# First 128 prompt tokens as a first group, with their expert rows gathered beside the recurrence

## The chip, the cores and the metric

The kernel runs on one core of a Trainium2 chip. The metric is device time in microseconds (us) of one execution, as the median of several runs. TensorE (PE in the profile) multiplies matrices, VectorE (DVE), ScalarE (ACT) and GpSimd (POOL) work on elements, SyncE (SP) issues most transfers; GpSimd issues the indirect ones. Each engine works through its own list of instructions in order; semaphores tie the lists together.

## The reference

One layer of a hybrid decoder is computed for 1024 prompt tokens and 32 sample tokens, 1024 features wide, in 32-bit floats:

```python
n1 = rmsnorm(x, norm_mix_g);  z = n1 @ w_in
y_r, shift_new, wkv_new = rwkv7_mix(z[..., :D_SHIFT], ...)   # 8 heads of 64; a scan over the tokens
y_p, pool_new = pool_mix(z[..., D_SHIFT:], ...)              # windows of 2, 4, 8, 16 tokens
h = x + concat([y_r, y_p]) @ w_out
h = h + peer_ffn(rmsnorm(h, norm_ffn_g), wq, keys, u_tab, v_tab)
gate = sigmoid(rmsnorm(h, norm_ple_g) @ ple_gate_w)
h = h + (p @ ple_w) * gate
y = rmsnorm(h, final_norm_g)

def peer_ffn(x):            # per token: 8 heads, 16 of 16384 experts each
    s1, s2 = q[:, :, 0] @ keys[0].T, q[:, :, 1] @ keys[1].T   # q = x @ wq
    v1, i1 = top_k(s1, 16);  v2, i2 = top_k(s2, 16)
    sc, ci = top_k(v1[..., :, None] + v2[..., None, :], 16)
    gate = softmax(sc)
    act = gelu(u_tab[expert] . x) * gate
    return sum(act * v_tab[expert])
```

The outputs are y for both kinds of tokens and the new shift, recurrence and pooling states.

## The kernel before

The 1056 tokens stand in one order of positions, the 32 samples first. Matrix products that need full precision split both operands into a high and a low part (`whi`, `wlo`, `yhi`, `ylo`) and do three passes.

Phase A projects all tokens through `w_in`, prepares the recurrence's inputs in `fd`, and makes the pooled features `yp_d`. Beside it, `wsplit` loads, splits and stores `wq` and the first half of `w_out`, in 40 half blocks, each through one buffer `sraw`. The recurrence (`bchunk`) takes the prompt in 16 chunks of 64 tokens, each handing a state `S` to the next (L613), with two chunks interleaved (`b_stream`); a chunk's masked factors are made on POOL (`ltm`, `X`), and its output goes to `y_d`. The samples have a chunk of their own.

After chunk 1, with the next chunks and the sample chunk merged in, `ple` (the embedding projection to `pl_d`) and `wpool` (the pooled half of `w_out` plus `x`, to `hx_d`) run for all tokens. Then the four token groups of `GROUPS` follow, 288, 256, 256 and 256 positions. `phase_c(gi)` does a group's output projection (TensorE passes at L661 to L663, then L704), norm (L718), `wq` (16 blocks) and key scores, which go to memory. `top` reads them back and finds the top 16 of each half, and `select` (inside `top`) the experts and gates.

The expert layer is done in two ways. Positions 0 to 671 (`GA` to `GB`) are dense: every expert row of `uT` and `vP` is applied to them in 128 blocks of 128 experts (L1075 through `ublock` and `vblock`, weights split at L1061 and L1063), each token's gates standing in a dense tile. `select` builds that tile in 168 steps of four tokens: two comparisons and products on VectorE (L875, L877, some on L878 or POOL), eight TensorE passes (L881), an eviction (L882); 32 tokens at a time go from `gst` to `g_d`. The other 384 positions (`GT`) are gathered in three tiles of 128 tokens: for each of 8 heads and 16 experts an indirect DMA (L1179) fetches one row of `u` per token, VectorE takes its product with the token (L1187), and after gelu and gate another fetches a row of `v`, which VectorE adds to `po` (L1196). Four `row` buffers take turns.

```python
for gi ... streams = [phase_c(step - 1), t_stream(step - 2), b_stream(...)]; merge(streams)
for col in range(0, GT, 128):       # top of the gather tiles, then the dense blocks,
    idx, gl = tinfo[GB + col]       # and each gather tile in turn
```

`merge` interleaves streams by their shares of steps done, `BC` says which chunks go with which group. What order each engine really gets is decided by a scheduler that works on its own estimate of the time; the tile pools with their buffer counts (`bufs`) set the waits. `gates` (in `Tail`) does the embedding gate at the end, for the dense part and then for the gathered one (`GH`), and `finish` writes `yT`.

Of the kernel before, what the change touches and what calls it, by code (L numbers as in the profile page):

```python
# [40 lines left out]
GROUPS = ((0, 288), (288, 544), (544, 800), (800, 1056))  # L41
# [20 lines left out]
def body(ctx, tc, io):  # L62
# [12 lines left out]
    hx_d = dram.tile([128, KB, T], F32, name="hx_d")  # L75
# [30 lines left out]
    keep = ctx.enter_context(tc.tile_pool(name="keep", bufs=1))  # L106
# [4 lines left out]
    pconst = phases.enter_context(tc.tile_pool(name="pconst", bufs=1))  # L111
# [8 lines left out]
    pbx = ExitStack()  # L120
# [44 lines left out]
    keys = pconst.tile([128, 2, 128], F32)  # L165
# [288 lines left out]

    maxn = max(b - a for a, b in GROUPS)
    def bchunk(c, sp=None):
# [7 lines left out]
        pos = 0 if smpl else NSMP + 64 * c  # L464
# [83 lines left out]
        def sample_s(k, o, last):  # L548
            for p in range(4):
                apb = sp[0][0].tile([128, NB, m], F32, name="apb", bufs=2)  # L550
# [42 lines left out]
        if smpl:  # L593
            po = out()
            for p in range(4):
                ps = PS(pst)
                for i, (k, s_) in enumerate(((1, vt), (0, u))):
                    uvb = sp_.tile([m, NB, 64], F32, name="uvb", bufs=2)
# [42 lines left out]
    def wblock(gi, b):  # L641
# [4 lines left out]
        for i in range(1 if b < KB else 2):  # L646
# [25 lines left out]
    def segs(gi):  # L672
        c0, c1 = GROUPS[gi]
        if c0 == 0:
            return ((0, NP, NSMP), (NSMP, 0, c1 - NSMP))
        return ((0, c0 - NSMP, c1 - c0),)
# [5 lines left out]
    def phase_c(gi):  # L682
# [7 lines left out]
        y = work.tile([128, 4, maxn], F32, name="y", tag="yp")  # L690
        nc.sync.dma_start(y[:, :, :n], y_d[:, :, c0:c1])
# [80 lines left out]
    def select(tk, col, m, V12, I12):  # L772
# [133 lines left out]

    def t_stream(gi):
        for t0, m in tiles_of(gi):
            if GA <= GROUPS[gi][0] + t0 < GB:
                yield from top(tk, GROUPS[gi][0] + t0, m)  # L910

    def t_len(gi):
        n = 0
        for t0, m in tiles_of(gi):
            if GA <= GROUPS[gi][0] + t0 < GB:
                n += 24 + m // 4
        return n
# [11 lines left out]
    BC = (0, 2, 4, 8, 12, 16)  # L929
# [23 lines left out]
    with tc.tile_pool(name="smp", bufs=1) as sp_, tc.tile_pool(name="hx", bufs=1) as hx:  # L953
# [17 lines left out]
        pT = sp_.tile([128, 2, T], F32, name="pT")  # L971
        nc.sync.dma_start(pT, io["p"])

        def split(pool, raw, shape, nm, bufs):
            hi = pool.tile(shape, F32R, name=nm + "hi", bufs=bufs)
            ACT(hi, raw, AF.Copy)
            lo = pool.tile(shape, F32R, name=nm + "lo", bufs=bufs)
            TT(lo, raw, hi.bitcast(F32), op=ALU.subtract)
            return hi, lo

        def ple():
            phi, plo = split(sp_, pT, [128, 2, T], "p", 1)
            for db in range(KB):
                wp = sp_.tile([128, 2, 128], F32, name="wp", bufs=2)
                nc.sync.dma_start(wp, io["ple_w"][db])
                hi, lo = split(sp_, wp, [128, 2, 128], "w", 2)
                pss = [PS("b3"), PS("b3"), PS("b2")]
                for k in range(2):
                    for w, x, first, last in ((hi, phi, k == 0, False), (hi, plo, False, False), (lo, phi, False, k == 1)):
                        for i, ps in enumerate(pss):  # L990
                            mm(ps[:, :XW], w[:, k, :], x[:, k, i * XW:(i + 1) * XW], start=first, stop=last)
                for i, ps in enumerate(pss):
                    o = sp_.tile([128, XW], F32, name="pout", bufs=2)
                    ACT(o, ps[:, :XW], AF.Copy)
                    nc.sync.dma_start(pl_d[:, db, i * XW:(i + 1) * XW], o)
                yield

        def wpool():
            yhi = hx.tile([128, PB, T], F32R, name="yhi")
            ylo = hx.tile([128, PB, T], F32R, name="ylo")  # L1000
            for g in range(PB):
                raw = hx.tile([128, T], F32, name="yraw", bufs=1)
                nc.sync.dma_start(raw, yp_d[:, g, :])
                ACT(yhi[:, g, :], raw, AF.Copy)
                TT(ylo[:, g, :], raw, yhi[:, g, :].bitcast(F32), op=ALU.subtract)
            for b in range(KB):
                raw = hx.tile([128, HK, 128], F32, name="wraw", bufs=2)
                nc.sync.dma_start(raw, io["w_out"][b, :, HK:, :])
                hi = hx.tile([128, HK, 128], F32R, name="whi", bufs=2)
                ACT(hi, raw, AF.Copy)  # L1010
                lo = hx.tile([128, HK, 128], F32R, name="wlo", bufs=2)
                TT(lo, raw, hi.bitcast(F32), op=ALU.subtract)
                for i in range(T // XW):
                    cs = slice(i * XW, (i + 1) * XW)
                    x = hx.tile([128, XW], F32, name="x", bufs=3)
                    nc.sync.dma_start(x, io["x"][:, b, cs])
                    ps = PS("b2")
                    mm3(ps, [(hi, lo)], (yhi[:, :, cs], ylo[:, :, cs]), XW)
                    TT(x, ps[:, :XW], x, op=ALU.add)
                    nc.sync.dma_start(hx_d[:, b, cs], x)  # L1020
                    yield
# [10 lines left out]
    ws = phases.enter_context(tc.tile_pool(name="ws", bufs=2))  # L1032
    mv = phases.enter_context(tc.tile_pool(name="mv", bufs=1))
    work = phases.enter_context(tc.tile_pool(name="wc", bufs=1))
    tk = phases.enter_context(tc.tile_pool(name="tk", bufs=1))
# [3 lines left out]
    it = gp.tile([128, EB, TC], F32, name="gst", bufs=2)[:, :, 0:4]  # L1039
# [9 lines left out]
    NPRE = 7  # L1049
# [38 lines left out]
    CL = [0, 24, 24, 24, 24]  # L1088
    for step in range(1, NG + 1):
        streams = []  # L1090
        if step < NG:
            c_ = BC[step + 1:step + 3]
            streams.append((b_len(*c_), b_stream(*c_)))
        if 0 <= step - 2 < NG:
            streams.append((t_len(step - 2), t_stream(step - 2)))
        if 0 <= step - 1 < NG:
            streams.append((CL[step], phase_c(step - 1)))
        if step == NG:
            for _ in streams[0][1]:
                pass  # L1100
            gstack.close()
            gqp = ctx.enter_context(tc.tile_pool(name="gqp", bufs=2, side="right", reuse_waits="tile"))
            streams = [streams[1], (NPRE, upre())]
        merge(streams)
        if step == NG - 1:
# [9 lines left out]
    for col in range(0, GT, 128):  # L1115
        with tc.high_priority(offset=LOW if col else 0):
            for _ in top(tk, GB + col, min(128, GT - col)):
                pass
    phases.close()
# [5 lines left out]
    rstack = ExitStack()  # L1125
    rows = rstack.enter_context(tc.tile_pool(name="rows", bufs=1, reuse_waits="tile"))
# [43 lines left out]
    for col in range(0, GT, 128):  # L1170
        m = min(128, GT - col)
# [42 lines left out]
    def square(acc, src, k, sq):  # L1214
        if k == 0:
            ACT(acc, src[:, 0, :], AF.Square)
            return
        ACT(sq, src[:, k, :], AF.Square)
# [15 lines left out]
    class Tail:  # L1234
# [4 lines left out]
        def prep(self):  # L1239
            for k in range(KB):  # L1240
                scaled(self.src[:, k, :], *self.xs[k], k)
# [8 lines left out]
        def gates(self, sub, mul):  # L1250
            nxt = self.load(0, sub)
            for db in range(KB):
# [10 lines left out]
                yield TT(self.src[:, db, :], self.src[:, db, :], sg, op=ALU.add).ins  # L1263
                if db < KB - 1:
                    square(self.acc, self.src, db, self.tmp())
                else:
                    self.more = [self.tmp()]
                    ACT(self.more[0], self.src[:, db, :], AF.Square)

        def finish(self):  # L1270
            rstd_of(self.acc, self.parts, self.more)
            yield
            for s, n in self.parts:
                for k in range(KB):
                    o = self.src[:, k, s:s + n]
# [4 lines left out]
    def whl(n, dt):  # L1280
# [3 lines left out]
    td = Tail(OT, [(XH[:, k, :], XL[:, k, :]) for k in range(KB)], DP, GA, whl("wh", F32), whl("wl", F32),  # L1284
# [3 lines left out]
    rstack.close()  # L1288
    gh = ctx.enter_context(tc.tile_pool(name="gh", bufs=1, reuse_waits="tile"))
    GH = gh.tile([128, KB, GT], F32)  # L1290
    nc.sync.dma_start(GH, h2_d)
    tg = Tail(GH, [(whl("wh", F32R)[:, :GT], whl("wl", F32R)[:, :GT]) for _ in range(KB)], GP, GB,
              gh.tile([128, GT], F32, name="rg"), gh.tile([128, GT], F32, name="accg"),
              lambda: gh.tile([128, GT], F32, name="tg", bufs=6))
# [21 lines left out]
def layout(a):  # L1316
# [14 lines left out]
    p = np.concatenate([a["p_sample"][0].reshape(NSMP, PLE), a["p_prompt"][0, 0]], 0)  # L1331
# [47 lines left out]
```

## Time and profile before

| | |
|---|---|
| median of 3 runs | 3515.53 us (3499.31 to 3530.12) |
| profiled execution | 3494.25 us, span 3492.4 us |
| granted TensorE clock | 0.975 |
| TensorE busy | 3262.7 us (93%) |
| VectorE busy | 2675.0 us (77%) |
| GpSimd busy | 1769.3 us (51%) |
| ScalarE busy | 1179.8 us (34%) |
| memory traffic | 883.61 MB, mean 253 GB/s |

A row of the profile names a line, an engine, an operation and its tiles (out<-in), how often it ran, its busy time and the mean of one in ns, then the idle time of its engine before it and what ended that. A table by stretches gives start and end, the length, and for each engine the busy time and the number of instructions. Shares over the whole span hide that stages have different limits, so the stretches are to be read one by one.

### The profile page before, as it was taken

The numbers are of one execution on the slowest core, as the hardware profiler recorded it, in microseconds if no ns is written. First come the engines' busy times: TensorE is split into PE (matmuls) and PEld (weight loads), VectorE is DVE, ScalarE is ACT, GpSimd is POOL, SyncE is SP. The second block draws the span as 40 slices with busy tenths as digits, with TensorE's granted clock in tenths as the row PEclk, the third lists the DMA queues.
The fourth block names the chain that finished last, engine by engine and source line by source line (L and its number), as shares of the span: only waits on it lengthen the run. The fifth ranks groups of instructions, "written<-read, shape, count | busy, mean of one in ns | idle before, by whom it ended". The sixth has DMA issues, their size and how long they took to land.

```text
span 3492.4 us, 57600 instructions
## 1 busy us (share of the span) xinstructions
PE 3262.7 (93%) x21831; PEld 3150.6 (90%) x21831; DVE 2675.0 (77%) x5366; ACT 1179.8 (34%) x1776; POOL 1769.3 (51%) x1433
## 2 busy tenths in 40 slices
PE   8997998999999899999999999999999999999997
PEld 7876998989989788999999999999999999999997
DVE  6767333279999799978788778878888787788866
ACT  6452424345556455322122122122122212222243
POOL 5434234145465454156656555555555565555635
PEclk9998999999999899999999999999999999999999
DMA  5667645767767867479888888889898898898834
GB/s 177 213 197 177 185 134 148 213 174 231 210 194 212 282 199 258 131 278 318 308 315 307 306 320 311 313 318 317 314 321 315 307 312 308 301 318 313 311 123 132
DMA packets 467861, 883.61 MB, mean 253 GB/s; under 512 B 129280, under 2 KB 252416, under 8 KB 463104
## 3 DMA queue, kind: packets, MB, share of 16 engines
q1 hardware_dynamic: 356992, 477.24, 43.5%
q0 software_dynamic: 110592, 402.70, 32.6%
q8 instruction: 171, 2.80, 0.3%
q14 instruction: 106, 0.87, 0.1%
HBM read 759.22 MB, written 120.60 MB: 252 GB/s over the span
## 4 chain that ended last, share of the span: by engine, by line
DMA 26%; PE 22%; DVE 19%; issue 14%; POOL 11%; ACT 1%; SPq 0%; POOLq 0%; DVEq 0%; ACTq 0%
DMA row<-v,idx 14%; POOL row L1179 10%; DMA row<-u,idx 7%; PE pd L1075 7%; PE ps L881 2%; DVE ab L875 2%; PE ps L663 2%; PE ps L661 2%; DVE row L1187 2%; PE ps L662 2%; DVE elo L1063 1%; DVE po L1196 1%; PE ps L526 1%; DVE ab L877 1%; DMA sraw<-wq 1%
## 5 line engine op out<-in xcount | busy, mean ns | idle before, releaser
L1179 POOL DMA_INDIRECT row<-u,idx x384 | 534.9, 1393 | 387.9 <-DVE row L1187 248.4
L1179 POOL DMA_INDIRECT row<-v,idx x384 | 520.5, 1355 | 377.3 <-DVE po L1196 222.4
L1196 DVE SCALAR_TENSOR_TENSOR po<-row,act,po 128x1024 f32<-128x1024 f32 x381 | 488.8, 1283 | 152.6 <-DMA row<-v,idx 147.8
L1187 DVE SCALAR_TENSOR_TENSOR row<-row,xt 128x1024 f32<-128x1024 f32 x384 | 463.6, 1222 | 179.4 <-DMA row<-u,idx 177.8
L1075 PE MATMUL pd<-XH,elo 128*128 128x336 f32 x2176 | 524.9, 323 | 52.2 <-DVE elo L1063 49.3
L1061 ACT ACTIVATE ehi<-eraw 128x1024 fp32r<-128x1024 f32 x278 | 293.0, 1054 | 750.3 <-PE pd L1075 676.1
L1075 PE MATMUL pd<-wh,elo 128*128 128x336 f32 (+1 forms) x2112 | 509.5, 320 | 31.2 <-DVE elo L1063 30.9
L1075 PE MATMUL pd<-XH,ehi 128*128 128x336 f32 x2176 | 518.0, 319 | 4.1 <-DVE OT L1150 2.3
L1075 PE MATMUL pd<-XL,ehi 128*128 128x336 f32 x2176 | 519.5, 320 | 0.0
L1075 PE MATMUL pd<-wh,ehi 128*128 128x336 f32 (+1 forms) x2112 | 506.5, 319 | 8.7 <-DVE tg L1260 6.3
L1075 PE MATMUL pd<-wl,ehi 128*128 128x336 f32 (+1 forms) x2112 | 504.3, 318 | 0.0
L1075 PEld LDWEIGHTS pd<-XH,elo 128*128 128x128 f32 x2176 | 376.9, 191 | 64.4 <-DVE elo L1063 61.5
L1075 PEld LDWEIGHTS pd<-wh,elo 128*128 128x128 f32 x2112 | 362.1, 189 | 40.1 <-DVE elo L1063 39.4
L1075 PEld LDWEIGHTS pd<-XH,ehi 128*128 128x128 f32 x2176 | 377.7, 192 | 5.1 <-ACT wt L1081 2.5
L1075 PEld LDWEIGHTS pd<-XL,ehi 128*128 128x128 f32 x2176 | 376.7, 191 | 0.2
L1075 PEld LDWEIGHTS pd<-wh,ehi 128*128 128x128 f32 x2112 | 364.2, 189 | 10.5 <-issue 8.4
L1075 PEld LDWEIGHTS pd<-wl,ehi 128*128 128x128 f32 x2112 | 364.3, 189 | 0.0
L1063 DVE TENSOR_TENSOR elo<-eraw,ehi 128x1024 fp32r<-128x1024 f32 x257 | 317.9, 1237 | 11.7 <-ACT ehi L1061 6.3
L1140 ACT ACTIVATE wh<-wt 128x672 fp32r<-128x672 f32 x128 | 97.5, 766 | 662.1 <-DVE wt L1138 662.1
L881 PE MATMUL ps<-ab 128*128 128x128 f16 x1344 | 195.9, 295 | 25.0 <-DVE ab L877 12.0
L124 POOL TENSOR_TENSOR ab<-ab,e 128x512 f16<-128x512 f16 x110 | 128.4, 1169 | 172.2 <-DVE ab L877 130.7
L882 ACT ACTIVATE gst<-ps 128x512 f32<-128x512 f32 x168 | 179.5, 1103 | 94.4 <-PE ps L881 92.5
(499 smaller groups left out, 5962.7 us busy)
## 6 DMA issues: line engine op xcount, KB each, us to landing
eraw<-uT SPq DMA_DIRECT2D x128, 512.0 KB, 5.4
eraw<-vP SPq DMA_DIRECT2D x128, 512.0 KB, 5.7
g_d<-gst SPq DMA_DIRECT2D x21, 2048.0 KB, 8.4
gq<-g_d SPq DMA_DIRECT2D x32, 1344.0 KB, 9.4
whi<-wc_d SPq DMA_DIRECT2D x148, 256.0 KB, 4.4
wlo<-wc_d SPq DMA_DIRECT2D x148, 256.0 KB, 4.7
wc_d<-shi SPq DMA_DIRECT2D x40, 256.0 KB, 2.6
wc_d<-slo SPq DMA_DIRECT2D x40, 256.0 KB, 3.1
```

What stands on the lines that cost most here:

```text
L124: nc.gpsimd.tensor_tensor(out, a, b, op=op)
L661: mm(ps[:, :n], whi[:, kk, :], xhi[:, k, :n], start=k == 0, stop=False)
L662: mm(ps[:, :n], whi[:, kk, :], xlo[:, k, :n], start=False, stop=False)
L881: mm(ps[:, i * 128:(i + 1) * 128], ab[:, k, :, i], ab[:, 0, :, i], start=k == 2, stop=k == 1)
L882: ACT(st[:, :, t2:t2 + 4].rearrange("p e t -> p t e"), v3(ps, 128), AF.Copy, scale=1.0 / GS)
L1061: ACT(hi, raw, AF.Copy)
L1063: sub(lo, raw, hi.bitcast(F32), op=ALU.subtract)
L1075: mm(ps[:, a, :n], w_[:, k, :], x_[:, s:s + n], start=first, stop=last)
L1140: ACT(wh, wt_, AF.Copy)
L1179: nc.gpsimd.indirect_dma_start(out=r[:m], out_offset=None, in_=io[tab], in_offset=bass.IndirectOffsetOnAxis(ap=idx[:m, hh, k:k + 1], axis=0))
L1187: STT(r[:m], r[:m], 1.0, xt[:m], op0=ALU.mult, op1=ALU.mult, accum_out=pre[:m, k:k + 1])
L1196: STT(po[:m], r[:m], act[:m, k:k + 1], po[:m], op0=ALU.mult, op1=ALU.add)
```

## The change

`GROUPS` gets a fifth group. The prompt's first 128 tokens move from their place behind the samples to the last 128 positions, and their group, number 0, is the first to be worked on; the four behind it hold 288, 256, 256 and 128 positions. `phase_c(0)` runs alone after chunks 0 and 1; its tile is a gather tile (`ttiles` lets `t_stream(0)` do its `top`). The `rows` pool is opened before the recurrence, and the gather loop takes the tile at `GT - NE` first, so that the scheduler may place it early. The dense positions, the number of gathered tokens (384) and the blocks are as before.

`wpool` and `hx_d` are gone: `wsplit` splits all of `w_out` (48 half blocks in place of 40), and `phase_c` projects both halves itself and adds `x`. `ple` runs as a stream beside the recurrence, in the buffers of `phase_c`. `BC` moves chunks earlier: 2 to 5 with the samples, 6 to 9 with group 1, 10 to 13 with group 2, 14 and 15 with group 3. `gst` has one buffer instead of two, `ab` two instead of three, `apb` and `uvb` one instead of two, `NPRE` is 6 instead of 7, and `GH` lies in the `row` buffers.

```diff
-GROUPS = ((0, 288), (288, 544), (544, 800), (800, 1056))
+NE = 128
+GROUPS = ((T - NE, T), (0, 288), (288, 544), (544, 800), (800, T - NE))
...
-        for i in range(0, HK if b < KB else KB, HK):
+        for i in range(0, KB, HK):
...
+    def position(t):
+        return t + T - NE if t < NE else t - NE + NSMP
...
-        pos = 0 if smpl else NSMP + 64 * c
+        pos = 0 if smpl else position(64 * c)
...
-        for i in range(1 if b < KB else 2):
+        for i in range(2):
...
-        for d, s, L in segs(gi):
-            nc.sync.dma_start(h[:, :, d:d + L], hx_d[:, :, s:s + L])
...
-        for k in range(HK):
-            split(k, y[:, k, :n], yhi, ylo)
+        for part in range(2):
+            y = work.tile([128, 4, maxn], F32, name="y", tag="yp")
+            if part:
+                for d, s, L in segs(gi):
+                    nc.sync.dma_start(y[:, :, d:d + L], yp_d[:, :, s:s + L])
+                    nc.sync.dma_start(h[:, :, d:d + L], io["x"][:, :, s:s + L])
+            else:
+                nc.sync.dma_start(y[:, :, :n], y_d[:, :, c0:c1])
+            for k in range(HK):
+                split(part * HK + k, y[:, k, :n], yhi, ylo)
...
-            st = gp.tile([128, EB, TC], F32, name="gst", bufs=2)
+            st = gp.tile([128, EB, TC], F32, name="gst", bufs=1)
...
-                ab = gp.tile([128, 3, EB, 4], F16, name="ab", bufs=3)
+                ab = gp.tile([128, 3, EB, 4], F16, name="ab", bufs=2)
...
+    def ttiles(gi):
+        c0 = GROUPS[gi][0]
+        return [(c0 + t0, m) for t0, m in tiles_of(gi) if gi == 0 or GA <= c0 + t0 < GB]
+
     def t_stream(gi):
...
+        for pos, m in ttiles(gi):
+            yield from top(tk, pos, m)
...
-    BC = (0, 2, 4, 8, 12, 16)
+    BC = (0, 2, 6, 10, 14, 16)
...
+    keep = ctx.enter_context(tc.tile_pool(name="keep", bufs=1, reuse_waits="tile"))
+    rows = ctx.enter_context(tc.tile_pool(name="rows", bufs=1, reuse_waits="tile"))
...
+    for _ in phase_c(0):
+        pass
...
-        merge([(30, bchunk(-1, ((sp_, ssm), bmask, cmask, spads))), (b_len(*BC[1:3]), b_stream(*BC[1:3]))])
-        for st in (ple(), wpool()):
-            for _ in st:
-                pass
+        merge([(60, bchunk(-1, ((sp_, ssm), bmask, cmask, spads))), (b_len(*BC[1:3]), b_stream(*BC[1:3])), (KB + 1, ple()), (t_len(0), t_stream(0))])
...
-    NPRE = 7
+    NPRE = 6
...
+    for gi in range(1, NG):
+        streams = [(24, phase_c(gi))]
+        if gi > 1:
+            streams.append((t_len(gi - 1), t_stream(gi - 1)))
+        if gi < NG - 1:
+            c_ = BC[gi + 1:gi + 3]
             streams.append((b_len(*c_), b_stream(*c_)))
...
+    for pos in range(GB, T - NE, 128):
+        for _ in top(tk, pos, 128):
+            pass
...
-    for col in range(0, GT, 128):
-        m = min(128, GT - col)
+    for col in (GT - NE, *range(0, GT - NE, 128)):
+        m = 128
```

The changed kernel's lines that the prediction names: L616 is the state update (L613 before), L882 the first VectorE operation of a dense gate step (L875 before), L1156 the gather (L1179 before).

More of the change, by code (lines that the diff above doesn't have):

```diff
@@ L991, in ple @@
                             mm(ps[:, :XW], w[:, k, :], x[:, k, i * XW:(i + 1) * XW], start=first, stop=last)
+                o = work.tile([128, 4, maxn], F32, name="pout", tag="yp").rearrange("p a b -> p (a b)")[:, :T]
                 for i, ps in enumerate(pss):
-                    o = sp_.tile([128, XW], F32, name="pout", bufs=2)
-                    ACT(o, ps[:, :XW], AF.Copy)
-                    nc.sync.dma_start(pl_d[:, db, i * XW:(i + 1) * XW], o)
+                    ACT(o[:, i * XW:(i + 1) * XW], ps[:, :XW], AF.Copy)
+                nc.sync.dma_start(pl_d[:, db, :], o)
                 yield
[L998 to L1021, printed above, removed]
         spads = (sp_.tile([128, 4, 4, 64], F32, name="spd"), sp_.tile([64, 4, 4, 64], F32, name="slp"))
@@ L1038, in body @@
     iota16 = gp.tile([128, EB, 4], F16, name="iota16")
-    it = gp.tile([128, EB, TC], F32, name="gst", bufs=2)[:, :, 0:4]
+    it = gp.tile([128, EB, TC], F32, name="gst", bufs=1)[:, :, 0:4]
     nc.gpsimd.iota(it, pattern=[[1, EB], [0, 4]], base=0, channel_multiplier=0, allow_small_or_imprecise_dtypes=True)
@@ L1086, in upre @@
             yield
[L1088 to L1092, printed above, removed]
-            streams.append((b_len(*c_), b_stream(*c_)))
[L1094 to L1105, printed above, removed]
+    for gi in range(1, NG):
[4 more added lines that the diff above has]
+            c_ = BC[gi + 1:gi + 3]
+            streams.append((b_len(*c_), b_stream(*c_)))
+        else:
             nc.sync.dma_start(io["wkv_p"], S[-1])
@@ L1114, in body @@
             xs = [(XH[:, k, :], XL[:, k, :]) for k in range(KB)]
-    for col in range(0, GT, 128):
-        with tc.high_priority(offset=LOW if col else 0):
-            for _ in top(tk, GB + col, min(128, GT - col)):
-                pass
+            for _ in streams.pop()[1]:
+                pass
+            gstack.close()
+            gqp = ctx.enter_context(tc.tile_pool(name="gqp", bufs=2, side="right", reuse_waits="tile"))
+            streams.append((NPRE, upre()))
+        merge(streams)
+    for pos in range(GB, T - NE, 128):
+        for _ in top(tk, pos, 128):
+            pass
     phases.close()
@@ L1267, in gates @@
                     self.more = [self.tmp()]
[L1268 removed]
+                    ACT(self.more[0], self.src(db), AF.Square)
         def finish(self):
```

87 lines of the change are left out of this document (37 added, 50 removed).

## The prediction

> **What bounds the kernel now.** I read the page's head first, then its slices, then a table of busy time over six stretches that I cut at events of the program, then the lines of the engines that the stretches name.
>
> ```profile
> span 3492.4 us, 57600 instructions
> ...
> PE   8997998999999899999999999999999999999997
> ...
> DVE  6767333279999799978788778878888787788866
> ```
>
> TensorE is busy nearly everywhere, but VectorE changes: little to do in slices 5 to 8, full in slices 9 to 17, around 80% later. The cuts of the table are the first recurrence state (391), the first and the last step that builds dense gate tiles (772, 1363), and the start of the row gathers (1500):
>
> ```profile
> core 0: us, PE busy (x) PEld busy (x) DVE busy (x) ACT busy (x) POOL busy (x), PEclk, DMA share, GB/s
> 0.00:391.00 391.00, 336.60 (x1833) 298.63 (x1834) 260.06 (x279) 194.71 (x340) 166.15 (x145) 0.95 0.63 194
> 391.00:772.00 381.00, 363.93 (x2855) 344.42 (x2855) 151.78 (x497) 134.39 (x277) 125.13 (x129) 0.99 0.60 166
> 772.00:1363.00 591.00, 545.35 (x4306) 518.05 (x4306) 553.98 (x2115) 327.26 (x504) 309.89 (x305) 0.95 0.75 223
> 1363.00:1500.00 137.00, 133.08 (x896) 131.54 (x896) 128.03 (x596) 49.86 (x70) 39.16 (x46) 0.99 0.47 155
> 1500.00:3300.00 1800.00, 1714.05 (x10912) 1692.96 (x10911) 1451.62 (x1746) 394.10 (x481) 1043.03 (x760) 0.99 0.89 313
> 3300.00:3492.00 192.00, 169.69 (x1038) 164.95 (x1036) 129.54 (x138) 79.52 (x106) 85.90 (x51) 0.96 0.45 146
> ```
>
> The events that I cut at have these first and last starts:
>
> ```profile
> L613 DVE TENSOR_TENSOR S<-ps,S x16: 394/413/425, 391.2 to 1162.8; 128x256 f32<-128x256 f32 x16
> ...
> L875 DVE TENSOR_TENSOR ab<-iota,e x168: 659/682/2708, 771.8 to 1363.4; 128x1024 f16<-128x1024 f16 x168
> ```
>
> So from 391 to 772 TensorE sets the time (364 of 381 us) and VectorE is 40% busy. From 772 to 1363 both are nearly full: 545 and 554 of 591. From 1500 on TensorE sets the time again (1714 of 1800, or 95%) with VectorE at 81%. The gathers, which this change moves, all lie in that last stretch, behind TensorE.
>
> ```profile
> L1179 POOL DMA_INDIRECT row<-u,idx x384 | 534.9, 1393 | 387.9 <-DVE row L1187 248.4
> L1179 POOL DMA_INDIRECT row<-v,idx x384 | 520.5, 1355 | 377.3 <-DVE po L1196 222.4
> L1196 DVE SCALAR_TENSOR_TENSOR po<-row,act,po 128x1024 f32<-128x1024 f32 x381 | 488.8, 1283 | 152.6 <-DMA row<-v,idx 147.8
> L1187 DVE SCALAR_TENSOR_TENSOR row<-row,xt 128x1024 f32<-128x1024 f32 x384 | 463.6, 1222 | 179.4 <-DMA row<-u,idx 177.8
> ...
> L1187 DVE DVE_READ_ACCUMULATOR row<-row,xt 128x1 f32 x384 | 31.4, 82 | 0.0
> ...
> PE pd L1075 <- DVE elo L1063: 78.2, 57, 4.8
> ```
>
> A gathered row costs VectorE 1.222 + 0.082 us for u or 1.283 for v, so 1.29 on the mean. What TensorE loses to the gathers there is small: 78.2 us of waits for weight splits queued behind them on VectorE (the last row, the waits of 1500 to 3300).
>
> **The order after the change.** The instruction order that the build fixes for each engine tells where the moved work stands. VectorE meets its first gathered row after four of the 16 recurrence updates. It has passed 134 of the early tile's 256 rows by the first dense gate step (L882, L875 before) and 271 rows by the last; the other 497 are consumed by the time 81 of the 128 expert blocks are gated. All 16 recurrence chunks now stand before the first dense gate step (8 before), and on TensorE 384 of the 12864 expert and gate passes stand before the last one (288 before). Engines run in order, so this holds on the chip.
>
> **Start to the first recurrence state.** The split of all of w_out adds 8 load-split-store rounds to 40. The chain of waits has these rounds follow each other through one buffer, some 6.7 us apart:
>
> ```profile
> 239.98 3.11 DMA sraw<-wq
> ...
> 246.67 2.71 DMA sraw<-wq
> ```
>
> At most 8 x 6.7 = 54 us. In the new order ten of the splits stand behind the clearing of the recurrence's pads on POOL, so most lies beside projection and first chunks; I take 10, with 0 and 54 as ends. 391 + 10 = 401.
>
> **Recurrence stretch, to the first dense gate step.** TensorE passes are costed by how they follow each other:
>
> ```profile
> 2445.46 65.73 PE pd L1075 x426
> ...
> 1001.08 0.28 PE L663 MATMUL ps<-hi,wlo 128*128 128x256 f32 x1
> 1001.19 0.28 PE L661 MATMUL ps<-hi,whi 128*128 128x256 f32 x1
> 1001.31 0.28 PE L662 MATMUL ps<-lo,whi 128*128 128x256 f32 x1
> 1001.43 0.28 PE L663 MATMUL ps<-hi,wlo 128*128 128x256 f32 x1
> ...
> 824.20 1.05 PE L521 MATMUL ps<-Y,ltm 128*128 128x128 f32 x8
> ```
>
> 336 columns follow every 0.154 us, 256 columns every 0.117 to 0.12, and eight plain 128-column passes take 1.05 us, one every 0.11. From the first two, 288 columns are 0.133 and 352 are 0.161. A split-weight pass of only 128 columns is not in the trace. A line through 256 and 336 would give 0.063; the plain passes say 0.11 is what a pass with a new weight costs at least; twice that, 0.22, is my upper end. I take 0.112, the same width. Summed so, the old stretch is 368 us of passes in 381 us. The new one has 14 chunks instead of 7 (350 us with sampling, 192 before), group 0 at 128 columns (576 x 0.112 = 65), group 1 at 288 (576 x 0.133 = 77), a third of the next group (192 x 0.119 = 23), the embedding projection (23) and small ones (24): 562 us. At the old ratio that is 562 x 381/368 = 582. VectorE has 413 us here by row means, 134 x 1.29 = 173 of it gathered rows, so it does not bind, but it runs in order: when a row is late, the recurrence behind it is late. In the gather stage that cost (177.8 + 147.8)/768 = 0.42 us a row, 134 x 0.42 = 56 us if all of it hits the chain and nothing if slack takes it. I take 38: 620.
>
> The row took 6.2 us from issue to landing, with four buffers in turn:
>
> ```profile
> DMA to landing us min/median/max: 4.2/6.2/11.8
> ```
>
> The Trainium skill, "DMA: Bandwidth & Descriptors", section "Anatomy of one DMA — SWDGE (gpsimd) path", gives about 2 us and bytes at 436 GB/s, an estimate of 3.2 us for this 512 KB; the trace says 6.2 at 313 GB/s of other traffic. By the page's figure the wait terms (38 here, 29 below) vanish and the time would be 67 us less; I keep the trace.
>
> **Dense gate stretch.** This decides. The old 591 us held 554 of VectorE work. The new stretch holds the same 168 steps and, by row means, 612 us of VectorE work beside gathers where the old held 603 (top-k of more gather tokens for the last recurrence chunks): 554 x 612/603 = 562. To it come 271 - 134 = 137 rows x 1.29 = 177: 739. TensorE has only 417 us of passes left here, so it cannot hide that. With the old 37 us of idle, and half of 137 x 0.42 = 58 for rows not landed, 805. No idle at all gives 739, all of the wait 834.
>
> The single output buffer is a cost that I leave at nothing:
>
> ```profile
> g_d<-gst SPq DMA_DIRECT2D x21, 2048.0 KB, 8.4
> ```
>
> 21 stores of 8.4 us are 176 us for which the next 32 tokens' evictions must wait; the VectorE work between stores (739/21 = 35 us) covers it, if the order has other work there. Two "ab" buffers instead of three are covered in the same way.
>
> **From the last dense gate step to the end.** Old: 3492 - 1363 = 2129. 96 more passes are already done: -15. 47 of 128 blocks see no gather: 47/128 of the 1800 - 1714 = 86 us of TensorE idle is 32, and of the 1% that the granted clock lacks 6. 2129 - 15 - 38 = 2076. All the idle gone is 2010, nothing gained 2129.
>
> **Sum.** 401 + 620 + 805 + 2076 = 3902 us of span, against 3492.4. The profiled execution took 3494.25, 1.85 outside the span, and lies 0.6% under the median of 3515.53. So 3904 for a like execution and 3928 scaled to the median; I give 3910, 11% slower. In short: 350 us of VectorE work leave a stage where TensorE hid them for one where VectorE is the bound, the extra group adds 61 us of passes, and 38 come back.
>
> **Rivals.**
> - *The gathers fit into VectorE's idle time, not slower.* One mechanism: from 391 to 1363 VectorE idles 229 + 37 = 266 us, the early rows need 271 x 1.29 = 350; if all idle is filled, the last gate step comes 84 later, at 1447, and with every TensorE idle gone behind it (2010), 3457. It decides if the last gate step comes before about 1450. Against it: the first row stands behind four chunks, and the order puts 137 rows into the full stretch. 4%.
> - *TensorE clock.* At half clock the dense gate stretch's 417 us of passes become 834, above 805, and the gate steps wait for TensorE: about +30 there, and +40 in the recurrence: 3980. For it: the granted clock was 0.95 from 772 to 1363 and 0.99 where TensorE was fuller; against, no row of a stretch shows under 0.95. 12%. The Trainium skill, "TensorE: Matmul & The Clock Gate", section "Part 1: The HAM clock gate (the "warmup" mystery)", says the clock halves after an idle window of some 3.4 us until a busy one; with TensorE half idle it speaks against the change.
> - *Store of the gate tile exposed, or 128-column passes at 0.22.* Half of 176 is +88: 3998; the passes of group 0 add 576 x 0.108 = 62: 3972 (the last group's lie under VectorE). 14% together.
> - *The early gather is not early* (rows late in the queue): then only the 61 us of passes are new, 3492 + 61 = 3553, slower; the order rules it out, 2%.
>
> **Chances.** Forecast 67%, the others as given. Low: no waits, 391 + 565 + 754 + 2040 = 3750. High: 54 of splits, the slow passes or the store, 2110 behind: 4060. A measurement here tells about 1% from no change; only the first rival reaches that or beyond, and of its 4% I put 3 on faster and 1 on the same; 1 more for the same is left for what no case names: faster 0.03, same 0.02, slower 0.95.
>
> **What would show it.** Right: the S updates (L616) end near 1000 and before the first L882; L882 runs from near 1021 to near 1826 with VectorE over 90% and TensorE near 55%; the last gather (L1156) issues some 885 us before the end (47 blocks x 96 passes x 0.154 = 695, and a tail of 190); from there TensorE over 98%. Wrong: the last L882 before 1600, TensorE over 85% in that stretch, or a dense stage shortened by more than 120 us.

## The result, and the profile after

The changed kernel took 4007.33 us (median of 4 runs, 3983.53 to 4017.82), the kernel before 3519.87 beside it: a ratio of 1.138, with a 95% interval of 1.131 to 1.146. That lies in the predicted range (3750 to 4060, with 3910 as the time); the span of the profiled execution was 4016.1 us where the sum had said 3902.

The head and the slices of the page of the changed kernel:

```profile
span 4016.1 us, 59241 instructions
...
PE   8988898789866567787599999999999999999997
...
DVE  6673137666899899869778787788788433333355
...
PEclk9998798899977778556699999999999999999998
```

TensorE now has a trough in slices 12 to 20 with the granted clock at 0.5 to 0.8, just where VectorE is mostly full, and VectorE has little to do in the last fifth. The table of stretches of the changed kernel is cut at the same events as in the prediction (first state update 387, first and last dense gate step 1113 and 1932, last gather near 3140, last gated block 3826), and below it are the rows of the two events:

```profile
core 0: us, PE busy (x) PEld busy (x) DVE busy (x) ACT busy (x) POOL busy (x), PEclk, DMA share, GB/s
0.00:387.00 387.00, 326.86 (x1766) 285.36 (x1767) 248.23 (x267) 184.97 (x324) 164.24 (x140) 0.94 0.59 187
387.00:1113.00 726.00, 640.06 (x4758) 601.34 (x4757) 420.59 (x1046) 241.77 (x504) 399.98 (x377) 0.90 0.85 246
1113.00:1932.00 819.00, 562.13 (x3448) 515.51 (x3446) 734.21 (x2537) 271.67 (x395) 459.02 (x422) 0.69 0.79 259
1932.00:3140.00 1208.00, 1120.83 (x7112) 1105.79 (x7113) 958.90 (x1147) 269.42 (x329) 690.25 (x498) 0.97 0.87 309
3140.00:3826.00 686.00, 685.38 (x4464) 685.10 (x4463) 229.87 (x238) 163.44 (x187) 0.00 (x0) 1.00 0.29 97
3826.00:4016.00 190.00, 161.00 (x965) 154.98 (x963) 101.61 (x118) 72.23 (x97) 72.32 (x42) 0.93 0.31 100
```

```profile
L616 DVE TENSOR_TENSOR S<-ps,S x16: 403/423/425, 386.9 to 1116.1; 128x256 f32<-128x256 f32 x16
...
L882 DVE TENSOR_TENSOR ab<-iota,e x168: 658/686/3305, 1113.0 to 1931.6; 128x1024 f16<-128x1024 f16 x168
```

Set beside the sum: up to the first state 387 (401 said); recurrence stretch 726 (620 said, 381 before); gate stretch 819 (805 said, 591 before); from there to the end 2084 (2076 said, 2129 before). Of the 114 us that the span is over the sum, 106 are in the recurrence stretch. From the last gather to the last gated block TensorE is busy 685.4 of 686 us: the gather-free end of the dense stage is as tight as forecast. Behind the last gate step the change gains 45 us.

A sum that fits can still rest on the wrong cause. The experiments were made to take the supposed cause away.

### The profile page after: what moved, and what is told of

It is laid out like the page before. It is cut to its first block, busy times and chain, and to the rows that moved or that the text cites. A ratio compares the mean times of both kernels' runs of the same rounds, so it can differ in the third digit from the quotient of the medians.

```text
span 4016.1 us, 59241 instructions
## 1 busy us (share of the span) xinstructions
PE 3496.3 (87%) x22505; PEld 3348.1 (83%) x22505; DVE 2693.4 (67%) x5348; ACT 1203.5 (30%) x1835; POOL 1785.8 (44%) x1479
## 5 line engine op out<-in xcount | busy, mean ns | idle before, releaser
L1156 POOL DMA_INDIRECT row<-u,idx x384 | 500.8, 1304 | 412.1 <-DVE row L1164 241.3
L1156 POOL DMA_INDIRECT row<-v,idx x384 | 498.8, 1299 | 382.2 <-DVE po L1173 200.1
L1173 DVE SCALAR_TENSOR_TENSOR po<-row,act,po 128x1024 f32<-128x1024 f32 x381 | 510.9, 1341 | 137.5 <-DMA row<-v,idx 133.1
L1164 DVE SCALAR_TENSOR_TENSOR row<-row,xt 128x1024 f32<-128x1024 f32 x384 | 501.8, 1319 | 148.2 <-DMA row<-u,idx 147.3
L888 PEld LDWEIGHTS <-ab 128*128 128x128 f16 x1344 | 144.7, 125 | 252.9 <-DVE ab L884 107.5
L123 POOL TENSOR_TENSOR wh<-wh,wt 128x672 f32<-128x672 f32 x7 | 12.5, 1790 | 738.9 <-ACT wt L1195 738.9
L664 PE MATMUL ps<-hi,whi 128*128 128x256 f32 (+2 forms) x912 | 311.3, 344 | 23.1 <-DMA whi<-wc_d 12.2
```

Source lines behind the costliest of these rows:

```text
L123: nc.gpsimd.tensor_tensor(out, a, b, op=op)
L664: mm(ps[:, :n], whi[:, kk, :], xhi[:, k, :n], start=k == 0, stop=False)
L888: mm(ps[:, i * 128:(i + 1) * 128], ab[:, k, :, i], ab[:, 0, :, i], start=k == 2, stop=k == 1)
L1156: nc.gpsimd.indirect_dma_start(out=r[:m], out_offset=None, in_=io[tab], in_offset=bass.IndirectOffsetOnAxis(ap=idx[:m, hh, k:k + 1], axis=0))
L1164: STT(r[:m], r[:m], 1.0, xt[:m], op0=ALU.mult, op1=ALU.mult, accum_out=pre[:m, k:k + 1])
L1173: STT(po[:m], r[:m], act[:m, k:k + 1], po[:m], op0=ALU.mult, op1=ALU.add)
```

## The experiments

The theory (V) was the prediction's: the early rows put 350 us of VectorE work where VectorE sets the time. The rivals were that the rows' transfers crowd the DMA engines (D), that the single buffers pace the gate steps (B), and that the rest of the rebuild costs the time (R, later G for the order of the groups and P for the pooled projection inside them). A stretch's length below is from the first and last start of the rows shown.

**Gather the tile late.** The pool of row buffers is opened after the groups, all else as changed.

```diff
-    rows = ctx.enter_context(tc.tile_pool(name="rows", bufs=1, reuse_waits="tile"))
     ws = phases.enter_context(tc.tile_pool(name="ws", bufs=2, reuse_waits="tile"))
...
     dw = ctx.enter_context(tc.tile_pool(name="dw", bufs=1, reuse_waits="tile"))
+    rows = ctx.enter_context(tc.tile_pool(name="rows", bufs=1, reuse_waits="tile"))
```

> The changed kernel with one move: the pool of row buffers is opened only when the dense expert stage begins, so the early tile is gathered there like the others. Theory V (the gathers took 350 us of VectorE time out of a stage where TensorE hid it into one where VectorE sets the time): the stretch from the first recurrence state to the last dense gate step falls from 1545 us to about 1070, the dense stage grows back to about 2130, the span comes to about 3590, 2 to 4% over the kernel before. Rival R (the rest of the rebuild costs the time: fifth group, pooled projection inside the groups, single buffers): it stays over 3850.

Measured: 3820.75 us, ratio 1.090 (1.085 to 1.095). The stretches of its profile:

```profile
387.00:943.00 556.00, 515.31 (x3791) 487.31 (x3792) 196.52 (x822) 175.86 (x388) 174.14 (x203) 0.90 0.63 178
943.00:1665.00 722.00, 608.47 (x4414) 571.86 (x4413) 584.75 (x2339) 315.77 (x492) 302.14 (x323) 0.82 0.68 202
```

V had forecast 3590. With no gather anywhere near it, the first gate step still comes at 943 instead of 772, and the 168 gate steps take 722 us instead of 591 although VectorE is busy only 585 of them (81%). So the early gather, on top of the rest, is worth 1.138 - 1.090, about 170 us of the 487, and the larger part is the rebuild. R, with "over 3850", forecast a little too much.

**No early transfers.** The early tile multiplies the token rows instead of fetched rows.

```diff
+        early = col == GT - NE
         def gather(tab, hh, k):
+            if early and tab == "v":
+                return xt
             r = rows.tile([128, D], F32, name="row", bufs=NROW)
+            if early:
+                return r
...
-                STT(r[:m], r[:m], 1.0, xt[:m], ...
+                STT(r[:m], (xt if early else r)[:m], 1.0, xt[:m], ...
```

> The changed kernel, but the early tile fetches no rows: its 256 VectorE products are done at full width on the token rows already there (its expert output is left out). Theory V: VectorE's load stays, so the last dense gate step still comes after 1750 and the span stays at 3850 to 3950. Rival D (the 134 MB of row transfers crowd the DMA engines, which were 0.89 to 0.98 busy from 630 to 1113 us, and make weights and rows late): the span falls by over 250, to about 3700 or less. If both count, the recurrence stretch gives back the 106 us by which it was longer than predicted, and the gate stretch nothing.

Measured: 3866.61 us in one run. The first gate step came at 1069, the gate stretch took 721 us, the rest 2075:

```profile
391.00:1069.00 678.00, 597.67 (x4107) 555.96 (x4107) 555.88 (x1207) 211.94 (x442) 259.02 (x221) 0.85 0.57 164
1069.00:1790.00 721.00, 577.12 (x4100) 543.70 (x4098) 584.73 (x2372) 300.42 (x459) 306.64 (x320) 0.77 0.66 201
```

The span is where V put it, but this run does not decide. With nothing to wait for, the scheduler put all 256 products ahead of the first gate step (VectorE 556 of 678 us), so the gate stretch lost its rows to the place before it. What it shows is that a gate stretch without products again takes 721 us, as in the late gather, at 81% of VectorE.

**No early products.** All rows are fetched, but the early tile's products work on 8 of 1024 elements.

```diff
+                w_ = 8 if col == GT - NE else D
-                STT(r[:m], r[:m], 1.0, xt[:m], ...
+                STT(r[:m, :w_], r[:m, :w_], 1.0, xt[:m, :w_], ...
...
-                    STT(po[:m], r[:m], act[:m, k:k + 1], po[:m], ...
+                    STT(po[:m, :w_], r[:m, :w_], act[:m, k:k + 1], po[:m, :w_], ...
```

> The changed kernel, but the early tile's 256 products work on 8 of 1024 elements (its expert output is left out), while all its rows are still fetched. Theory V: 256 x 1.2 us of VectorE time are gone, most of it from the two full stretches: the gate stretch falls from 819 to about 680, the span to 3700 to 3800. Rival D: the transfers stay and so does the time, over 3950.

Measured: 3993.11 us in one run. Some 310 us of VectorE work gone gave 14 us, no more than the changed kernel's own runs differ (3983 to 4018). Up to the last gate step it gave 118 (1814 instead of 1932), and most of that was lost behind it:

```profile
1062.00:1814.00 752.00, 538.22 (x3429) 498.52 (x3428) 578.44 (x2348) 265.59 (x393) 404.64 (x425) 0.72 0.87 289
1814.00:1960.00 146.00, 53.28 (x327) 51.90 (x326) 113.53 (x303) 22.98 (x33) 84.19 (x69) 0.65 0.78 262
```

```profile
PE pd L1059 <- ACT wt L1065: 91.3, 1, 91.3
```

The second answer is what TensorE waited for from 1814 to 1950: one wait of 91.3 us for a gelu on ScalarE, which by its own waits (27.7 us for a softmax, 13.9 for indices) sat in order behind results that VectorE still owed. The changed kernel has the same wait with 24.5 us. V in its simple form falls: if VectorE's load alone set the gate stretch, it would have shrunk by 137 x 1.2 = 164 us, and it shrank by 67.

D is not settled by these two runs: its forecast came true here (over 3950) and failed in the run before (3700 or less), and V's did the reverse. The recurrence stretch took 726 us with both transfers and products, 678 without the transfers, 676 without the products and 556 without either (the late gather). Taking one away alone gives back little, and each run has an order of its own, so how transfers, products and order share the price of the early gather stays open.

**Two output and three operand buffers again, with the late gather.**

```diff
-            st = gp.tile([128, EB, TC], F32, name="gst", bufs=1)
+            st = gp.tile([128, EB, TC], F32, name="gst", bufs=2)
...
-                ab = gp.tile([128, 3, EB, 4], F16, name="ab", bufs=2)
+                ab = gp.tile([128, 3, EB, 4], F16, name="ab", bufs=3)
```

> As the late gather, with two output buffers of the gate tile and three operand buffers again, as before the change. Theory V: within 1% of the late gather, since VectorE work lies between the stores. Rival B (the single output buffer, 77 us of TensorE waits behind its eviction in the changed kernel's gate stretch): 60 to 100 us faster than the late gather.

Measured: 3769.73 us, ratio 1.074 (1.068 to 1.079), 51 us under the late gather.

```profile
943.00:1556.00 613.00, 542.93 (x4026) 514.39 (x4026) 544.46 (x2101) 296.47 (x460) 291.69 (x304) 0.86 0.76 224
1556.00:1647.00 91.00, 65.37 (x403) 64.75 (x402) 47.12 (x251) 26.94 (x40) 23.01 (x23) 0.71 0.47 156
```

The gate stretch falls from 722 to 613, almost its old length; half of the gain is given back in a hole before the dense stage, as in the run above (TensorE busy 65 of 91 us).

**The kernel before with single buffers.** The reverse edit, nothing else.

> The kernel before with one output buffer of the gate tile instead of two and two operand buffers instead of three, nothing else. Theory B (the buffers pace the gate steps): the gate stretch grows from 591 us to about 700, as between the two late-gather kernels (722 and 613), and the span by 80 to 110: 3580 to 3600. Theory V (only VectorE's load counts): within 20 us of 3492.

Measured: 3587.78 us, ratio 1.022 (1.020 to 1.025).

```profile
394.00:773.00 379.00, 360.11 (x2822) 340.99 (x2821) 151.84 (x496) 133.95 (x275) 124.98 (x129) 0.99 0.59 167
773.00:1463.00 690.00, 592.46 (x4661) 558.73 (x4660) 610.17 (x2419) 342.75 (x532) 333.25 (x332) 0.90 0.68 203
```

B holds, in a second kernel: the gate stretch grows from 591 to 690 us, and the stretch ahead of it is unchanged. Not all of the 99 us is waiting, since the longer stretch took in 355 more passes and 56 us more VectorE work; but the span grew by 95, so the price is real. TensorE's waits at the gate passes (L881) tell where it arises:

```profile
PE ps L881 <- DVE ab L877: 40.9, 34, 3.5
PE ps L881 <- ACT gst L882: 23.3, 7, 5.9
```

These two were 12.0 and 3.6 us with the old buffers.

**The kernel before with the pooled projection inside the groups.** `wpool` and `hx_d` go, `wsplit`, `wblock` and `phase_c` are edited as in the change; groups, order and buffers stay.

> The kernel before with the pooled half of the output projection done inside each group (all of w_out split, pooled features and x loaded by the group, no stage of its own), four groups as before. Theory G (the late start of the gate steps comes from the order of the groups): the first gate step stays near 772 and the span within 40 us of 3492. Rival P (work that filled TensorE early is gone and the groups are longer): the first gate step comes after 850 and the span is over 3560.

Measured: 3592.24 us, ratio 1.022 (1.017 to 1.027).

```profile
389.00:792.00 403.00, 371.76 (x2772) 348.37 (x2771) 140.54 (x509) 137.44 (x290) 140.09 (x148) 0.92 0.60 166
792.00:1408.00 616.00, 562.95 (x4424) 532.73 (x4423) 568.18 (x2096) 328.38 (x509) 327.08 (x321) 0.93 0.76 227
1408.00:1582.00 174.00, 159.04 (x1061) 156.81 (x1060) 115.32 (x581) 54.78 (x79) 33.75 (x39) 0.94 0.45 153
```

Between G and P: the first gate step is late by only 20 us, but the gate stretch takes 25 more and the way from there to the first gather 174 instead of 137; the span is 100 us longer with hardly any new time of passes (384 more at 0.12 us in place of 288 at 0.161). The filler work that `wpool` gave TensorE is gone: the granted clock ahead of the gates is 0.92 instead of 0.99.

**The first group second.** From the late gather with two buffers, `phase_c(0)` follows `phase_c(1)` in one stream instead of standing ahead of all. Its `top` moves too, from beside the samples' chunk to behind the groups, with that of the other gather tiles.

```diff
-    for _ in phase_c(0):
-        pass
...
+        def c10():
+            yield from phase_c(1)
+            yield from phase_c(0)
-        streams = [(24, phase_c(gi))]
+        streams = [(48, c10()) if gi == 1 else (24, phase_c(gi))]
```

> The late gather with two buffers (3770 us), but the group of the first 128 tokens is worked on behind the first dense group instead of ahead of it. Theory G: the first gate step moves from 943 towards 850, since 64 us of passes at full clock, more at half clock, no longer stand ahead of it; what is left over 772 is the two chunks more that the dense group waits for; span 3670 to 3710. Rival P: the first gate step stays near 940 and the span near 3770.

Measured: 3838.14 us, ratio 1.093 (1.088 to 1.098): slower.

```profile
389.00:839.00 450.00, 413.81 (x3079) 387.11 (x3079) 150.28 (x523) 151.75 (x321) 148.01 (x161) 0.91 0.58 155
839.00:1133.00 294.00, 273.80 (x2214) 263.88 (x2213) 234.87 (x744) 149.99 (x253) 147.75 (x146) 0.94 0.77 215
1133.00:1289.00 156.00, 123.50 (x881) 114.06 (x879) 92.10 (x429) 49.13 (x93) 45.21 (x55) 0.87 0.74 237
```

The first gate step did move, from 943 to 839, as G said. But the small group now stood between the first and the second dense group, and the gate steps, 72 for the first and 64 for the second, almost stopped in the middle: 14 steps in 156 us. So the small group delays the gates by some 100 us in both places: it is a whole round of projection, norm, queries and scores in series, and feeds no gate step. The span, 3832 us, is longer than both forecasts. A part of that may be the moved `top`, which now stands behind the last gate step: the 132 us there held one TensorE wait of 69 us.

**The gate passes twice.** In the changed kernel each gate step's eight passes are done twice.

> The changed kernel with each gate step's eight TensorE passes done twice (same result). Theory B (each step goes around through two operand buffers, VectorE to POOL to TensorE and back, so TensorE's time per step is on the path): 168 x 0.94 = 158 us at most, a gate stretch of 900 to 980. Theory V (VectorE's load sets the stretch, TensorE has room): within 30 us of 819. Rival C (the half clock makes TensorE the bound there): the fuller engine gets more clock, and the stretch is not longer.

Measured: 4051.96 us in one run; gate stretch 857.

```profile
1110.00:1967.00 857.00, 645.57 (x4776) 607.34 (x4774) 746.56 (x2547) 274.11 (x394) 454.28 (x426) 0.79 0.76 248
```

159 us more of passes at full clock cost 38 us and brought the clock from 0.69 to 0.79. None of the three forecasts fits: V allowed 30 us, B meant at least 81, C none, though the clock did rise as C said. TensorE's time is not what sets that stretch; some of the steps do wait for it.

**One of the two buffers.** The late gather with three operand buffers and one output buffer.

> The late gather with three operand buffers of a gate step, but one output buffer. It tells the two buffers apart: if the output buffer with its 2 MB store paces the steps, the gate stretch stays near 722 us (span near 3810); if the operand buffers do, it falls to about 613 (span near 3770).

Measured: 3784.25 us in one run.

```profile
951.00:1601.00 650.00, 576.91 (x4183) 551.42 (x4183) 538.55 (x2135) 300.73 (x469) 293.54 (x306) 0.83 0.74 217
```

With the runs above, 722, 650 and 613 us: in the gate stretch the third operand buffer is worth 72, the second output buffer 37. Of the span (3809.8, 3782.6, 3769.6) they give 27 and 13, since the stages behind lose some of it again. TensorE's waits for operands at the gate passes fell from 56 to 8 us with the third operand buffer; those for the eviction went from 20 to 32.

**The first group's passes twice**, in the changed kernel.

> The changed kernel with the 576 passes of the first 128-token group done twice (same result), 65 us more of passes at full clock. Theory L (before the first gate step the new kernel waits in serial chains, 726 us for 561 us of passes, so TensorE has room): the first gate step moves by less than 30 us from 1113. Theory T (TensorE's time, at half clock for 151 us there, sets it): it moves by 65 to 130.

Measured: 4066.98 us in one run.

```profile
387.00:1163.00 776.00, 695.76 (x5336) 659.47 (x5335) 411.87 (x1049) 241.39 (x503) 409.58 (x374) 0.92 0.78 228
```

The first gate step came 50 us later for 65 us of passes, between L and T and nearer to T: in spite of its gaps TensorE has little room in that stretch, at least where this group stands.

**A way to beat both.** Since buffers pace the gate steps, the kernel before got a fourth operand buffer (and `NPRE` 6 to make room), then also all low products on GpSimd.

> The kernel before with four operand buffers of a gate step instead of three (six early blocks instead of seven make room). Theory B (buffers pace the gate steps): the gate stretch falls from 591 to 560 to 580, the span by 10 to 30. Theory V: VectorE is 94% busy there already, no change over 10 us.

> The same with all low products of the gate steps on GpSimd instead of two of three: 56 x 0.61 = 34 us less on VectorE, 66 more on GpSimd (310 of 591 busy). If VectorE's load sets the gate stretch, it and the span fall by 25 to 35 us (1%); if the chain of a step does, GpSimd's slower product makes it 10 to 40 us longer.

Measured: 3537.19 us, ratio 1.010 (1.006 to 1.013), and 3538.1 us, ratio 1.010 (1.007 to 1.014).

```profile
771.00:1353.00 582.00, 526.05 (x4149) 498.13 (x4149) 560.94 (x2081) 315.59 (x490) 307.82 (x302) 0.93 0.74 217
1353.00:1522.00 169.00, 157.76 (x1059) 155.56 (x1057) 129.14 (x635) 57.23 (x83) 37.53 (x46) 0.95 0.49 161
```

The fourth buffer gave 9 us in the gate stretch, which is what V had said and less than B had (11 to 31), with VectorE 96% busy there. The way to the gathers gave back 32; whether the early block that was given up is behind that was not separated. With the low products on GpSimd the stretch was 617 us, within the forecast of the step's chain. VectorE was still busy 567 us of it, as other work took the place of the products, so this run shows only that the move does not pay. No version here beats the kernel before.

## Why the prediction was right, and where its steps were wrong

**The direction** was right for the reason given: the instruction order put 134 rows ahead of the first gate step and 137 between the gate steps, and TensorE sets the dense stage, so little could come back. The end took 2084 us for 2076 said. **The size** was right in part by luck. The cause that the prediction puts first, 350 us of VectorE work, is worth about 170 of the 487 us; the rest, some 315, is the rebuild, of which the sum had 10 us for the split, the passes of the extra group, and nothing for buffers and lost filler.

**The signs** named beforehand came out in part. The last gather was issued 881 us before the end (885 said), and VectorE was busy 90% of the gate stretch. But the S updates ended at 1116 instead of near 1000, with the last of the 16 behind the first gate step (1113), where the prediction had all of them ahead of it; and TensorE was busy 69% of the gate stretch instead of near 55%, because its passes ran in part at half clock.

**The split of all of w_out** (10 us, 0 to 54) cost nothing: the first state came at 387.

**The passes** were counted right: with each pass at its spacing at full clock they come to 561 us in the trace for the recurrence stretch, 562 said. The old stretch was not: counted in the same way it holds 349 us, and the 368 of the prediction are more than the 364 that TensorE was busy there. The narrow pass was chosen well at full clock. These are passes of the first group in the timeline of the changed kernel, first at half, then at full clock:

```profile
494.20 0.41 PE L665 MATMUL ps<-lo,whi 128*128 128x128 f32 x1
494.41 0.41 PE L666 MATMUL ps<-hi,wlo 128*128 128x128 f32 x1
...
526.21 0.28 PE L664 MATMUL ps<-hi,whi 128*128 128x128 f32 x1
526.32 0.28 PE L665 MATMUL ps<-lo,whi 128*128 128x128 f32 x1
```

0.11 us, as the plain 128-column passes had said; 0.21 at half clock.

**The recurrence stretch (620 said, 726 measured) is the step that failed.** The wrong term is the scale 381/368: it was taken from a stretch that the independent work of `wpool` kept full, and the change takes that cover away. Measured, a microsecond of passes took 726/561 = 1.29; counted in the same way it was 381/349 = 1.09 before. Without the early gather it is nearly as high, 556 us for 448 of passes (1.24), so the lost cover, more than the rows, is behind it; the pooled projection alone has it too, 403 for 334 (1.21). By these ratios the 582 us of the sum lack 32 for the miscounted old passes, 84 for the cover and the first group, and 28 for the early gather: 726 in all. The clock has its part: it was at half for 151 us (0.90 granted, 0.99 before), and TensorE was busy 640 us for its 561 of passes, where it had been 364 for 349. The term for late rows (38 us) was of the right size: the waits of VectorE there were

```profile
DVE row L1164 <- DMA row<-u,idx: 26.5, 12, 7.1
DVE po L1173 <- DMA row<-v,idx: 26.3, 20, 4.9
```

53 us for 134 rows, 56 said as the most. By the estimate from the Trainium skill, "DMA: Bandwidth & Descriptors", section "Anatomy of one DMA — SWDGE (gpsimd) path", they would vanish; the trace disagrees. In the gate stretch they did nearly vanish: 2.3 us of such waits, 29 said. (The 313 GB/s that the prediction sets beside the landing time are not other traffic: the rows themselves are 397 of the 563 MB moved from 1500 to 3300.)

**The gate stretch (805 said, 819 measured) was right in size by luck.** VectorE's load was 734 us, 739 said. The sum had 177 + 29 us for the rows and nothing for the buffers; measured are 97 and 109, the same 206. So "a cost that I leave at nothing", the single buffers, is the term that was mis-sized: 99 us by themselves in the old order, 109 in the new, and "covered in the same way" fails most, since the operand buffers are 72 of the 109. The reason given, VectorE work between the stores, does not cover it: each step goes from VectorE, for two of three low products over GpSimd, to TensorE before its operand buffer is free again. That it is this round that costs is argued; on record are the waits of TensorE at the gate passes, given above, while VectorE's own waits for them hardly fell with the third operand buffer (77 and 74 us). In the changed kernel the two costs lie over each other: 722 us with the buffers alone, 97 more with the gathers, not 177. Of the stretch's growth by 228, taken off in this order, 22 remain without either (613), about 109 are the buffers and 97 the rows.

**By parts of the change**, as far as runs separate them, in ratios to the kernel before: pooled projection inside the groups 1.022; with fifth group, embedding projection as a stream, chunk order and six early blocks, two buffers and late gather 1.074; single buffers 1.090; early gather 1.138. What is left open is how the 5% between the first two divide between the fifth group and the rest of the new order; the run that moved the group shows that it holds up the gates, but not the price of each piece. Whether early gathers with two buffers cost 97 or 177 us there was not tried.

**The rivals.** *Gathers fit into idle time*: out, the last gate step came at 1932. *TensorE clock*: the clock did fall as the rival said, to 0.69 in the gate stretch (half for 509 of 819 us), yet it did not become the bound of that stretch, as the doubled passes show. In the recurrence stretch it did cost (640 us busy for 561), and there the doubled passes found little room. By the rule of the Trainium skill on the clock gate ("TensorE: Matmul & The Clock Gate", section "Part 1: The HAM clock gate (the "warmup" mystery)") the clock halves after an idle window and returns after a busy one; the traces agree with the first half in the main, since the clock is lowest where TensorE idles most, but not with the second. The first of these stretches is from the late gather, the second from the changed kernel:

```profile
461.00:484.00 23.00, 23.00 (x116) 21.39 (x116) 2.25 (x5) 2.61 (x6) 2.64 (x4) 0.51 0.47 145
1641.00:1760.00 119.00, 96.55 (x529) 91.35 (x528) 107.01 (x488) 39.67 (x70) 52.63 (x64) 0.50 0.73 226
```

The clock stood at half while TensorE had no idle time at all, and through 119 us in which it was 81% busy. Most passes there are the 128-column ones of the two small groups and of the gate steps. Whether narrow passes keep the clock low was not tried; if they do, the small groups cost more than their passes at full clock. *Store exposed*: right in kind, but the output buffer is worth 37 us in place of 88, and the larger price, that of the operand buffers, is in no rival. *128-column passes at 0.22*: out at full clock (0.11), though at half clock they take 0.21. *Not early*: out, the first row was fetched at 629 us.

## What to carry to other kernels

Work moved into a stage that looks idle pays for whatever that stage's idle time was hiding: count the independent filler that the same change removes, and do not carry a stage's passes-to-time ratio over to one without its filler. A buffer count is a price of its own: hold the time around one buffer against the time between two uses, in order and engine by engine, before calling it covered. When a sum fits, take its largest term away on the chip; here the term was worth half of what it seemed, and another that had been put at nothing made the sum fit.

## What the runs showed of the hardware

A pass of two split operands with 128 columns follows every 0.112 us, against 0.119 with 256: a group half as wide saves hardly any TensorE time, so 576 narrow passes cost nearly what 576 passes of twice the width do. The granted clock fell to 0.69 over 819 us in which TensorE was still busy 69% by its records, and the 417 us of passes there took 562: a stage that starved TensorE also ran its passes at three quarters of full speed. Doubling the gate passes brought the clock to 0.79. And a full TensorE was not enough for the full clock: in the late gather it ran at 0.51 for 23 us (461 to 484) without any idle time.
